# Attention of a two-layer hybrid encoder: lower probabilities on two 64-column halves of TensorE, scores without a rescale, late convolution taps added by DMA

## The chip, the core and the metric

The kernel runs on one core of a Trainium2 chip. TensorE (PE; PEld is its weight load), VectorE (DVE), ScalarE (ACT), GpSimd (POOL) and SyncE (SP, which issues DMAs) each run their own queue in order. The metric is the device time of one execution in microseconds. The median of three runs before is 2212.58 us (2212.55 to 2213.03).

## What is computed

Two layers, each with multi-head latent attention beside a convolution module, then a gated feed-forward part with a short convolution. 1024 tokens, width 1024, 8 heads, head sizes 64 (plain) + 32 (rotary) for queries and keys and 64 for values. What matters here:

```python
sc = einsum("bqhd,bkhd->bhqk", qn, k_nope) + einsum("bqhr,bkr->bhqk", qr, k_rope)
p = softmax(sc * scale)                 # scale = 1 / sqrt(96)
y_attn = einsum("bqhk,bkhd->bqhd", p, v)
u = a * sigmoid(gt)                     # the convolution module, beside attention
u = dwconv(u, w_dw_conv) + b            # 31 taps, per channel
u = silu(layernorm(u))
y = concat([y_attn, u]) @ w_o
```

## The kernel before

Channels lie on partitions, tokens along the free dimension. A float32 factor is held as two parts, an upper and a lower one, and a product of two factors is three matmuls (upper x upper, upper x lower, lower x upper). In attention the parts are float16.

A layer has three stages: the projection (`project`), attention (`attention`) with the output product behind it, and the feed-forward part. Each has its own PSUM pool; in attention there are two wide tiles of two banks for scores (`wide`) and four single banks (`bank`) for turned probabilities and for outputs.

**Scales.** In the projection, sums of squares of weights and gains give powers of two by which queries and keys are scaled before they become float16. `query_scale` and `key_scale` work each out from a column of `qk`, on DVE after a tiny matmul with ones; `head_squares` squares the query and key weights on ACT. `score_scale` makes the factor `self.sback` that brings a score back to its true size.

**Attention** is written as 64 units per layer, n = 8 * head + query tile of 128 tokens. Unit n issues, in this order:
- `values` (L1841): one of four chunks of 256 keys of a group of 512 queries. The stationary operand `v` is 128 columns wide: 64 columns of upper values and 64 of lower ones. The odd heads have them the other way round. So `v` times the upper probabilities gives upper x upper on one half of the output's partitions and lower x upper on the other. With the lower probabilities `pt[1]` it gives upper x lower and, unused by the three-matmul rule, lower x lower. Four matmuls of 512 columns (two blocks of 128 keys by two parts). After the fourth chunk both halves of the bank `o` are scaled and added into `yt` (L1847 on ACT, L1848 on DVE).
- `turn` (L1818): eight transposes of probabilities into PSUM tiles `t`; ACT writes the upper part (L1820), DVE the lower part (L1821).
- `scores` (L1777) for the tile two units ahead: six matmuls of 512 columns, then on DVE the negated row maximum `mx` (L1779), multiplied by `sback` (L1780).
- `expo` (L1788) for the tile one unit ahead: ACT takes the exponential with `mx` as its bias and `sback` as its scale, with the row sums beside it.
- `agenda[n]`: side work. Among it are row sums turned by a transpose of 8 columns (`sr`, L1859), weight casts for the output product, and the late taps.

**Taps.** Of the 31 taps of the four blocks of 128 convolution channels, some are done in the projection; 50 of the first layer and 49 of the second are left to attention (`late`). `LATE_KINDS` gives, by half of the list and in turns of five, how each is done (`tap_late`): "act": two halves on ACT (L2009), then a DMA that adds the result to `conv` (L2017); "pool": one product on POOL (L2012), then such a DMA; "both": a product and an addition on POOL (L2012, L2015), no DMA. The DMAs are issued by POOL. `LATE_COST` spreads the taps over the first 56 units; only the ACT halves are tied to a unit, POOL works through its queue as it can. An addition to one `conv` block waits for the one before it. `conv_total` (L2023, POOL) sums the blocks in units 57 to 59, `conv_split` (L2027, ACT and DVE) makes parts of the sum in unit 64, and `lnp` (L2039, PE) takes its mean behind attention.

Of the kernel before, what the change touches and what calls it, by code (L numbers as in the profile page):

```python
# [49 lines left out]
P_GQ = 8  # L50
# [31 lines left out]
MANUAL = [E.PE, E.DVE, E.Activation, E.Pool, E.SP]  # L82
LATE_KINDS = (("act", "both", "pool", "act", "pool"), ("pool", "both", "pool", "pool", "pool"))
LATE_COST = {"act": 1.1, "pool": 3.5, "both": 4.8}
# [54 lines left out]
class Encoder:  # L139
# [420 lines left out]
    def project(self, l, carry):  # L560
# [14 lines left out]
        def gain_squares():  # L575
            nc.vector.memset(col(6), 0.0)
            for i, at, n in ((0, P_GQ, 3), (4, P_GKV, 2)):
                nc.scalar.activation(out=self.blk(f"gsq{l}{i}")[:, 0:n], in_=par[:, at:at + n], func=AF.Square, accum_out=col(i))

        def head_squares(name):  # L580
            hi = w[name][0]
            i = {"u0": 1, "u1": 2, "u2": 3, "k": 5}[name]
            nc.scalar.activation(out=self.blk(f"hsq{l}{name}", F16, tuple(hi.shape)), in_=hi.bitcast(F32), func=AF.Square, accum_out=col(i))

        def totals(at, n, name):
            ps = self.bank(f"{name}{l}", (128, n))
            nc.tensor.matmul(ps, self.ones, col(at, n), start=True, stop=True)
            return ps

        def query_scale():  # L590
            sums = totals(0, 4, "qt")
            nc.vector.tensor_reduce(out=col(0), in_=sums[:, 1:4], op=ALU.add, axis=AX.X)
            nc.vector.tensor_tensor(out=col(0), in0=sums[:, 0:1], in1=col(0), op=ALU.mult)
            self.half_exponent(col(1), col(0))
            self.power(col(2), col(1), -1.0, 199.0)

        def score_scale():
            self.power(col(3), col(1), 1.0, 55.0)
            self.power(col(4), col(5), 1.0, 50.0)
            nc.vector.scalar_tensor_tensor(out=col(7), in0=col(3), scalar=SCALE, in1=col(4), op0=ALU.mult, op1=ALU.mult)  # L600
            self.sback = col(7)

        def key_scale():
            nc.vector.tensor_copy(out=col(4, 3), in_=totals(4, 3, "kt"))
            nc.vector.scalar_tensor_tensor(out=col(4), in0=col(4), scalar=float(KVL), in1=col(5), op0=ALU.mult, op1=ALU.mult)
            nc.vector.tensor_tensor(out=col(4), in0=col(4), in1=col(6), op=ALU.add)
            self.half_exponent(col(5), col(4))
            self.power(col(6), col(5), -1.0, 204.0)
            launch(key_rope_end())
# [93 lines left out]
        def queries_norm():  # L703
            r, d = self.blk(f"rq{l}"), rooted("qroot")
            st["rq"] = r
            query_scale()
# [156 lines left out]
        scales = {1: lambda: st.update(squares=self.weight_squares(l, w["v"])),  # L863
                  2: lambda: (st.update(scale=self.scales(l, st.pop("squares"))), score_scale())}
        for j in range(4):
# [9 lines left out]
        def supply(now, turn=TURN):  # L875
            while coming and coming[0][1] <= now + LEAD:
                name, at = coming.pop(0)
                turning.append((name, at, self.cast(l, name)))
            while turning and turning[0][1] <= now + turn:
                name, at, e = turning.pop(0)  # L880
                w[name] = self.complete(*e)
                if name in ("u0", "u1", "u2", "k"):
                    head_squares(name)
# [856 lines left out]
    def attention(self, l, u, conv, away, spill, kvs, loaded, ahead, wo, begun):  # L1740
# [28 lines left out]
        def scores(n):  # L1769
# [9 lines left out]
            nc.vector.tensor_reduce(out=mx, in_=ps, op=ALU.max, axis=AX.X, negate=True)  # L1779
            nc.vector.tensor_scalar(out=mx, in0=mx, scalar1=self.sback, scalar2=None, op0=ALU.mult)  # L1780
            st["s"][qt] = ps, mx

        def expo(n):
# [3 lines left out]
            p = self.tmp("b" if qt % 4 == 3 else "wr", f"p{l}_{h}_{qt}")  # L1787
            nc.scalar.activation(out=p, in_=ps, func=AF.Exp, bias=mx, scale=self.sback,  # L1788
                                 accum_out=st["sums"][:, qt:qt + 1])
# [36 lines left out]
        def values(group, c, n):  # L1826
# [11 lines left out]
            pt = st["pt"][gg][c // 2]  # L1838
            for s in range(2):
                for i in range(2):  # L1840
                    nc.tensor.matmul(po, v[2 * c + i][:, h // 2, e, :], pt[s][:, 2 * (c % 2) + i, :],  # L1841
                                     start=(c == 0 and i == 0 and s == 0), stop=(c == 3 and i == 1 and s == 1))
            if c < 3:
# [314 lines left out]
```

## Time and profile before

| | |
|---|---|
| profiled execution | 2213.27 us |
| its span | 2211.5 us |
| median of the runs | 2212.58 us |
| granted TensorE clock | 0.999 |
| projection of layer 0, until about | 198 us |
| attention of layer 0, steady part | 217.5 to 395.2 us |
| its end, until the first output products | 413.3 us |
| attention of layer 1 begins about | 1305 us |

In the page, a row of a group reads: line, engine, operation, output <- inputs by the program's names with buffer numbers left out, shapes, count, then busy time and mean duration of one, then idle time ahead and what ended it. A matmul's end is modelled, and it overlaps the next; what a matmul costs in a stream is the distance from start to start, and that is what the chain of waits shows. In a row of a time line, the first number is the start in microseconds from the start of the span, the second the length. The stage rows give busy time of PE, PEld, DVE, ACT and POOL, then the granted clock, the mean busy share of the 16 DMA engines and GB/s.

### The profile page before, as it was taken

How to read it: one execution, taken by the hardware profiler on the slowest of the kernel's cores; microseconds unless marked ns; L12 is line 12 of the kernel's file. 1: busy time of each engine (PE TensorE's matmuls, PEld its weight loads, DVE VectorE, ACT ScalarE, POOL GpSimd, SP SyncE). 2: the span in 40 equal slices, each digit the busy share in tenths (PEclk: the TensorE clock that was granted, in tenths of full speed). 3: DMA queues.
4: the chain of work that ended last, by engine and by line, in shares of the span. 5: the costliest groups of instructions: out<-in, count | busy, mean ns of one | idle time of the engine just before them, and what ended most of it. 6: DMA issues, size and time to landing. Idle time of an engine off the chain costs nothing.

```text
span 2211.5 us, 29902 instructions
## 1 busy us (share of the span) xinstructions
PE 2200.3 (99%) x10774; PEld 1320.3 (60%) x10774; DVE 1857.6 (84%) x2644; ACT 1487.9 (67%) x2223; POOL 593.5 (27%) x546
## 2 busy tenths in 40 slices
PE   9999999999999999999999999999999999999998
PEld 8887666784444444644488876667744444446445
DVE  6989999778988887787859789997788888878877
ACT  5455988745898886554623669887468987865544
POOL 1221799511111111000012227983111111110000
PEclk9999999999999999999999999999999999999999
DMA  6886878955588886554558958778646888856533
GB/s 192 164 178 176 161 159 160 289 142 120 126 249 258 221 258 160 191 167 154 166 137 166 194 148 174 157 178 241 167 103 146 257 238 238 239 141 220 183 117 120
DMA packets 163269, 400.96 MB, mean 181 GB/s; under 512 B 22144, under 2 KB 30192, under 8 KB 163120
## 3 DMA queue, kind: packets, MB, share of 16 engines
q0 software_dynamic: 67136, 154.28, 37.7%
q1 hardware_dynamic: 95696, 244.24, 32.3%
q8 instruction: 84, 1.38, 0.3%
q10 hardware_dynamic: 288, 0.53, 0.1%
q14 instruction: 65, 0.53, 0.1%
HBM read 270.75 MB, written 69.66 MB: 154 GB/s over the span
## 4 chain that ended last, share of the span: by engine, by line
PE 90%; DVE 6%; ACT 2%; issue 1%; DMA 1%; SPq 0%; DVEq 0%; ACTq 0%
PE p L1268 36%; PE pd L1513 16%; PE po L1002 7%; PE s L1777 7%; PE o L1841 5%; PE t L1818 5%; PE pa L239 2%; PE pg L239 2%; DVE conv L1995 2%; PE pg L557 2%; PE pq L239 1%; PE pkv L239 1%; PE pn L239 1%; PE pa L557 1%; PE pv L1753 1%
## 5 line engine op out<-in xcount | busy, mean ns | idle before, releaser
L1268 PE MATMUL p<-b,w 128*128 128x512 f16 x3696 | 804.0, 379 | 0.0
L1268 PEld LDWEIGHTS <-w 128*128 128x128 f16 x3696 | 361.5, 99 | 427.4 <-issue 1.1
L1513 PE MATMUL pd<-ab,wd 128*128 128x512 f16 (+2 forms) x1920 | 404.2, 373 | 0.0
L1159 POOL DMA_DIRECT2D wu<-in_w_up x176 | 152.9, 882 | 744.2 <-DVE w L1232 539.8
L1513 PEld LDWEIGHTS <-wd 128*128 128x128 f16 x1656 | 161.9, 98 | 179.3 <-issue 0.5
L1777 PE MATMUL s<-k,q 96*128 96x512 f16 x768 | 186.9, 379 | 0.0
L1232 DVE SCALAR_TENSOR_TENSOR w<-wu,wf,w 128x512 f16<-128x512 f32 (+1 forms) x216 | 177.3, 835 | 3.9 <-ACT w L1229 3.9
L1821 DVE SCALAR_TENSOR_TENSOR pt<-t,pt 128x512 f16<-128x512 f32 x256 | 163.4, 679 | 14.7 <-ACT pt L1820 11.5
L2012 POOL TENSOR_TENSOR late<-gate,par 128x1016 f32<-128x1016 f32 (+11 forms) x79 | 170.9, 2163 | 0.0
L1229 ACT ACTIVATE w<-wu,wf 128x512 f16<-128x512 f32 (+1 forms) x216 | 165.3, 784 | 0.0
L1820 ACT ACTIVATE pt<-t 128x512 f16<-128x512 f32 x256 | 139.4, 597 | 38.3 <-PE t L1818 36.7
L1788 ACT ACTIVATE p<-s,mx,qk 128x1024 f32<-128x1024 f32 x128 | 155.4, 1214 | 2.1 <-DVE mx L1780 1.1
L1779 DVE TENSOR_REDUCE mx<-s 128x1 f32<-128x1024 f32 x128 | 155.3, 1213 | 0.0
L1502 ACT ACTIVATE ab<-ac,ds 128x512 f16<-128x512 f32 x108 | 75.7, 718 | 108.2 <-DVE ac L1417 72.8
L1995 DVE SCALAR_TENSOR_TENSOR conv<-gate,par,conv 128x1009 f32<-128x1009 f32 (+14 forms) x110 | 139.9, 1275 | 3.3 <-ACT conv L657 0.6
L1818 PEld LDWEIGHTS t<-ident,p 128*128 128x128 f32 x1024 | 119.6, 141 | 28.5 <-ACT p L1788 2.1
L1818 PE MATMUL t<-ident,p 128*128 128x128 f32 x1024 | 134.4, 273 | 1.7 <-ACT p L1788 1.0
L1841 PE MATMUL o<-pt,v 128*128 128x512 f16 x512 | 131.3, 379 | 0.0
L1725 DVE SCALAR_TENSOR_TENSOR o<-zg,par,o 128x1023 f32<-128x1023 f32 x88 | 112.8, 1282 | 8.9 <-ACT o L1719 7.4
L1276 DVE SCALAR_TENSOR_TENSOR zg<-p,wf,zg 128x512 f32<-128x512 f32 x72 | 54.1, 751 | 72.2 <-PE p L1268 62.3
L1777 PEld LDWEIGHTS <-q 96*128 96x128 f16 x768 | 74.2, 97 | 64.6 <-issue 2.1
L1725 DVE SCALAR_TENSOR_TENSOR v<-zv,par,v 128x1023 f32<-128x1023 f32 x88 | 112.2, 1277 | 0.0
(2190 smaller groups left out, 3978.7 us busy)
## 6 DMA issues: line engine op xcount, KB each, us to landing
wu<-in_w_up SPq DMA_DIRECT2D x98, 512.0 KB
wu<-in_w_up POOLq DMA_DIRECT2D x176, 256.0 KB, 4.8
sd<-in_w_down SPq DMA_DIRECT2D x44, 512.0 KB
ws<-sd SPq DMA_DIRECT2D x44, 512.0 KB
act<-v SPq DMA_DIRECT2D x36, 512.0 KB
ac<-act SPq DMA_DIRECT2D x72, 256.0 KB
wo<-in_w_o POOLq DMA_DIRECT2D x64, 256.0 KB, 7.2
x_mix<-y SPq DMA_DIRECT2D x32, 256.0 KB
```

Source lines behind the costliest of these rows:

```text
L1229: nc.scalar.activation(out=t, in_=src, func=AF.Copy, scale=scale[f])
L1232: nc.vector.scalar_tensor_tensor(out=t, in0=src, scalar=scale[f], in1=hi, op0=ALU.mult, op1=ALU.subtract)
L1268: nc.tensor.matmul(ps, w[p][:, k * 128:(k + 1) * 128], b[:, q], start=(i in (1, 5, 2) and k == 0 and t == 0), stop=(k == 3 and t == 2), sk ...
L1513: nc.tensor.matmul(ps[t, m][:, cs], w[i, j][p][:, m * 128:(m + 1) * 128], b[:, q, cs], start=(i in (1, 5, 2) and j == 0 and s == 0), stop= ...
L1725: self.nc.vector.scalar_tensor_tensor(out=o[:, a:b], in0=z[:, at + a:at + b], scalar=self.par[l][:, tap:tap + 1], in1=o[:, a:b], op0=ALU.m ...
L1777: nc.tensor.matmul(ps[:, cs], q[0:96, i, qs], k[0:96, j, cs], start=(s == 0), stop=(s == 2))
L1788: nc.scalar.activation(out=p, in_=ps, func=AF.Exp, bias=mx, scale=self.sback, accum_out=st["sums"][:, qt:qt + 1])
L1818: nc.tensor.transpose(tp[:, i, qi * 128:(qi + 1) * 128], st["p"][2 * qp + qi][:, kt * 128:(kt + 1) * 128], self.ident)
L1821: nc.vector.scalar_tensor_tensor(out=lo, in0=tp, scalar=P_SCALE, in1=hi, op0=ALU.mult, op1=ALU.subtract)
L1841: nc.tensor.matmul(po, v[2 * c + i][:, h // 2, e, :], pt[s][:, 2 * (c % 2) + i, :], start=(c == 0 and i == 0 and s == 0), stop=(c == 3 and ...
L1995: self.nc.vector.scalar_tensor_tensor(out=y[:, lo:hi], in0=u[:, lo + s:hi + s], scalar=self.tap(l, j, t), in1=y[:, lo:hi], op0=ALU.mult, o ...
L2012: self.nc.gpsimd.tensor_tensor(out=p[:, lo:hi], in0=u[:, lo + s:hi + s], in1=self.tap(l, j, t).broadcast_to([128, hi - lo]), op=ALU.mult)
```

## The change

Three edits.

1. `values`: the two matmuls with the lower probabilities take only the 64 columns of upper values. The first block of 128 keys goes into partitions 0 to 63 of the bank, the second into 64 to 127. The lower x lower products are left out, and the upper x lower ones are spread over both halves, which are added at the end as before.
2. Queries are no longer scaled by a power of two of their own: `key_scale` also makes the factor `col(2)` for them, the keys' scale taken back and 1/sqrt(96) put in. The scores leave TensorE in their true size; `mx` is not multiplied, and the exponential has no scale. `query_scale`, `score_scale` and the squares of the three query weights go.
3. `LATE_KINDS`: in both halves of the list "both" becomes "pool"; in the second half the first of each five turns from "pool" to "act".

```diff
-LATE_KINDS = (("act", "both", "pool", "act", "pool"), ("pool", "both", "pool", "pool", "pool"))
+LATE_KINDS = (("act", "pool", "pool", "act", "pool"), ("act", "pool", "pool", "pool", "pool"))
...
-        def query_scale():
-            sums = totals(0, 4, "qt")
-            nc.vector.tensor_reduce(out=col(0), in_=sums[:, 1:4], op=ALU.add, axis=AX.X)
-            nc.vector.tensor_tensor(out=col(0), in0=sums[:, 0:1], in1=col(0), op=ALU.mult)
-            self.half_exponent(col(1), col(0))
-            self.power(col(2), col(1), -1.0, 199.0)
...
         def key_scale():
-            nc.vector.tensor_copy(out=col(4, 3), in_=totals(4, 3, "kt"))
+            sums = self.bank(f"kt{l}", (128, 3))
+            nc.tensor.matmul(sums, self.ones, col(4, 3), start=True, stop=True)
+            nc.vector.tensor_copy(out=col(4, 3), in_=sums)
...
-            self.power(col(6), col(5), -1.0, 204.0)
+            self.power(col(6), col(5), -1.0, 200.0)
+            self.power(col(2), col(5), 1.0, 54.0)
+            nc.vector.tensor_scalar(out=col(2), in0=col(2), scalar1=SCALE, scalar2=None, op0=ALU.mult)
...
             nc.vector.tensor_reduce(out=mx, in_=ps, op=ALU.max, axis=AX.X, negate=True)
-            nc.vector.tensor_scalar(out=mx, in0=mx, scalar1=self.sback, scalar2=None, op0=ALU.mult)
...
-            nc.scalar.activation(out=p, in_=ps, func=AF.Exp, bias=mx, scale=self.sback,
+            nc.scalar.activation(out=p, in_=ps, func=AF.Exp, bias=mx,
...
-            for s in range(2):
-                for i in range(2):
-                    nc.tensor.matmul(po, v[2 * c + i][:, h // 2, e, :], pt[s][:, 2 * (c % 2) + i, :],
-                                     start=(c == 0 and i == 0 and s == 0), stop=(c == 3 and i == 1 and s == 1))
+            for i in range(2):
+                nc.tensor.matmul(po, v[2 * c + i][:, h // 2, e, :], pt[0][:, 2 * (c % 2) + i, :],
+                                 start=(c == 0 and i == 0), stop=False, skip_group_check=True)
+            for i in range(2):
+                nc.tensor.matmul(po[i * 64:i * 64 + 64], v[2 * c + i][:, h // 2, e, main], pt[1][:, 2 * (c % 2) + i, :],
+                                 start=False, stop=(c == 3), skip_group_check=True)
```

On TensorE, one unit of values between scores and turns (first layer, head 0, second group; `pt_10` is a tile of lower probabilities; each matmul has a weight load ahead of it). Before:

```order
L1777 MATMUL s_1_1_1962<-k_1_1704,q_1_1703 128x512
L1841 LDWEIGHTS v_0_1608
L1841 MATMUL o_0_1_1976<-pt_00_1876,v_0_1608 128x512
...
L1841 MATMUL o_0_1_1976<-pt_10_1877,v_0_1608 128x512
...
L1818 MATMUL t_0_32_1981<-ident,p_0_6_1899 128x128 x2
L1818 MATMUL t_0_32_1981<-ident,p_0_7_1935 128x128 x2
```

And now:

```order
L1760 MATMUL s_1_1_1938<-k_1_1686,q_1_1685 128x512
L1822 LDWEIGHTS v_0_1593
L1822 MATMUL o_0_1_1949<-pt_00_1854,v_0_1593 128x512
...
L1825 MATMUL o_0_1_1949<-pt_10_1855,v_0_1593 64x512
...
L1800 MATMUL t_0_32_1954<-ident,p_0_6_1876 128x128 x2
L1800 MATMUL t_0_32_1954<-ident,p_0_7_1911 128x128 x2
```

The order and the number of matmuls stay (each `o` row stands twice, once per block of keys); those with `pt_10` write 64 partitions instead of 128.

On DVE, in the same stretch (`mx` the maximum, `pt_1x` the lower probabilities). Before:

```order
L1779 TENSOR_REDUCE mx_2_5_2412<-s_2_5_2405 128x1
L1780 TENSOR_SCALAR mx_2_5_2412<-mx_2_5_2412,qk_84 128x1
L1821 SCALAR_TENSOR_TENSOR pt_11_2326<-t_2_12_2429,pt_01_2325 128x2x256
L1821 SCALAR_TENSOR_TENSOR pt_11_2326<-t_2_13_2436,pt_01_2325 128x2x256
L1779 TENSOR_REDUCE mx_2_6_2450<-s_2_6_2443 128x1
L1780 TENSOR_SCALAR mx_2_6_2450<-mx_2_6_2450,qk_84 128x1
```

And now:

```order
L1803 SCALAR_TENSOR_TENSOR pt_11_2289<-t_2_13_2394,pt_01_2288 128x2x256
L1762 TENSOR_REDUCE mx_2_6_2408<-s_2_6_2401 128x1
L1845 RECIPROCAL rs_1_2419<-sr_1_2417 8x128
L1803 SCALAR_TENSOR_TENSOR pt_10_2433<-t_2_20_2427,pt_00_2432 128x2x256
L1803 SCALAR_TENSOR_TENSOR pt_10_2433<-t_2_21_2438,pt_00_2432 128x2x256
L1762 TENSOR_REDUCE mx_2_7_2452<-s_2_7_2445 128x1
```

The `TENSOR_SCALAR` behind each maximum is gone; nothing else moved.

On POOL, the first late taps of the first layer (`late_j_t` is tap t of block j, `conv_j` the sum). Before:

```order
L2012 TENSOR_TENSOR late_0_19_1758<-gate_0_416,par_63 128x1020
L2015 TENSOR_TENSOR conv_0_475<-conv_0_475,late_0_19_1758 128x1020
L2012 TENSOR_TENSOR late_1_19_1798<-gate_1_477,par_63 128x1020
L2017 DMA conv_1_539<-late_1_19_1798 128x1020
...
L2017 DMA conv_3_854<-late_3_17_1827 128x1022
L2012 TENSOR_TENSOR late_3_18_1903<-gate_3_786,par_63 128x1021
L2015 TENSOR_TENSOR conv_3_854<-conv_3_854,late_3_18_1903 128x1021
```

And now:

```order
L1996 TENSOR_TENSOR late_0_19_1739<-gate_0_414,par_63 128x1020
L2001 DMA conv_0_473<-late_0_19_1739 128x1020
L1996 TENSOR_TENSOR late_1_19_1742<-gate_1_475,par_63 128x1020
L2001 DMA conv_1_537<-late_1_19_1742 128x1020
...
L2001 DMA conv_3_852<-late_3_17_1806 128x1022
L1996 TENSOR_TENSOR late_3_18_1880<-gate_3_784,par_63 128x1021
L2001 DMA conv_3_852<-late_3_18_1880 128x1021
```

Each addition on POOL has become a DMA issue. Over both layers 79 such issues become 99, the 20 additions and 10 of the 79 products on POOL go, and the halves of taps on ACT go from 40 to 60.

More of the change, by code (lines that the diff above doesn't have):

```diff
@@ L576, in gain_squares @@
             nc.vector.memset(col(6), 0.0)
-            for i, at, n in ((0, P_GQ, 3), (4, P_GKV, 2)):
-                nc.scalar.activation(out=self.blk(f"gsq{l}{i}")[:, 0:n], in_=par[:, at:at + n], func=AF.Square, accum_out=col(i))
+            nc.scalar.activation(out=self.blk(f"gsq{l}")[:, 0:2], in_=par[:, P_GKV:P_GKV + 2], func=AF.Square, accum_out=col(4))
         def head_squares(name):
             hi = w[name][0]
[L582 to L588, printed above, removed]
-        def query_scale():
-            sums = totals(0, 4, "qt")
-            nc.vector.tensor_reduce(out=col(0), in_=sums[:, 1:4], op=ALU.add, axis=AX.X)
-            nc.vector.tensor_tensor(out=col(0), in0=sums[:, 0:1], in1=col(0), op=ALU.mult)
-            self.half_exponent(col(1), col(0))
-            self.power(col(2), col(1), -1.0, 199.0)
[L597 to L601, printed above, removed]
+            nc.scalar.activation(out=self.blk(f"hsq{l}{name}", F16, tuple(hi.shape)), in_=hi.bitcast(F32), func=AF.Square, accum_out=col(5))
         def key_scale():
-            nc.vector.tensor_copy(out=col(4, 3), in_=totals(4, 3, "kt"))
+            sums = self.bank(f"kt{l}", (128, 3))
+            nc.tensor.matmul(sums, self.ones, col(4, 3), start=True, stop=True)
+            nc.vector.tensor_copy(out=col(4, 3), in_=sums)
             nc.vector.scalar_tensor_tensor(out=col(4), in0=col(4), scalar=float(KVL), in1=col(5), op0=ALU.mult, op1=ALU.mult)
@@ L705, in queries_norm @@
             st["rq"] = r
-            query_scale()
             for s, p in zip(HALVES, self.spread(d, f"rq{l}", HALVES, self.bank)):
@@ L863, in project @@
         scales = {1: lambda: st.update(squares=self.weight_squares(l, w["v"])),
-                  2: lambda: (st.update(scale=self.scales(l, st.pop("squares"))), score_scale())}
+                  2: lambda: st.update(scale=self.scales(l, st.pop("squares")))}
         for j in range(4):
@@ L881, in supply @@
                 w[name] = self.complete(*e)
-                if name in ("u0", "u1", "u2", "k"):
+                if name == "k":
                     head_squares(name)
```

## The prediction

> **What bounds the kernel now.** I read the page's head and its chain first, then the chain of waits inside attention in order of time, then the busy time by stretch.
>
> ```profile
> span 2211.5 us, 29902 instructions
> PE 2200.3 (99%) x10774; PEld 1320.3 (60%) x10774; DVE 1857.6 (84%) x2644; ACT 1487.9 (67%) x2223; POOL 593.5 (27%) x546
> PE 90%; DVE 6%; ACT 2%; issue 1%; DMA 1%; SPq 0%; DVEq 0%; ACTq 0%
> ```
>
> TensorE is busy all the time and makes up 90% of the chain. So only work taken off TensorE can shorten this kernel, and only as long as nobody else falls behind. The change works on attention, so here is its chain in the first layer (start, length, engine and line):
>
> ```profile
> 217.68 0.88 PE t L1818 x6
> ...
> 301.58 1.30 PE s L1777 x6
> 302.87 0.87 PE o L1841 x4
> 303.74 0.87 PE t L1818 x8
> 304.61 1.30 PE s L1777 x6
> ...
> 395.24 0.91 PE t L1818 x8
> ```
>
> One unit of attention is scores (six matmuls, 1.30 us), values (four, 0.87) and turns (eight transposes, 0.87): 3.03 us, back to back, with no other engine in the chain. A streamed 512-column matmul thus costs 0.87/4 = 0.216 us. The busy time by stretch (PE, PEld, DVE, ACT, POOL, then clock, DMA share, GB/s; the last row is the values line alone, PE and PEld):
>
> ```profile
> 3.00:198.00 195.00, 194.44 (x878) 160.20 (x878) 167.61 (x211) 99.65 (x121) 39.71 (x48) 1.00 0.76 176
> 217.50:282.00 64.50, 64.33 (x378) 39.42 (x379) 60.15 (x93) 61.56 (x109) 50.91 (x35) 1.00 0.81 160
> 217.50:395.20 177.70, 177.53 (x1051) 109.45 (x1051) 167.49 (x256) 156.03 (x273) 154.31 (x103) 1.00 0.80 161
> 217.50:395.20 177.70, 59.92 (x232) 22.60 (x232) 1.00 0.80 161
> ```
>
> The steady stretch holds 232/4 = 58 units in 177.7 us, 3.06 each. The others are close behind: DVE 94%, ACT 95% up to 282, POOL 87%, DMA 0.80.
>
> **Values on two column halves.** The third and fourth product of a unit become two of 64 columns, one into partitions 0 to 63 of the bank, one into 64 to 127. If both stream together, four slots become three: 0.216 us a unit, 58 x 0.216 = 12.5 us a layer. No row of before shows two column tiles at once, so the saving lies between nothing and 0.216, and below nothing if switching between tile shapes costs. [...]
>
> ```profile
> 245.93 1.46 PE L1777 MATMUL s<-k,q 96*128 96x512 f16 x6
> 247.01 0.09 PEld L1859 LDWEIGHTS sr<-ident,sums 128*8 128x8 f32 x1
> 247.23 0.28 PE L1859 MATMUL sr<-ident,sums 128*8 128x128 f32 x1
> 247.23 0.64 PEld L1841 LDWEIGHTS <-v 128*128 128x128 f16 x4
> 247.34 1.02 PE L1841 MATMUL o<-pt,v 128*128 128x512 f16 x4
> ```
>
> Six scores from 245.93 at 0.216 end their streaming at 247.23, and the small tile starts right there; its weights were loaded at 247.01 under the last full matmul. The values start 0.11 later, what a transpose takes anyway (0.87/8). So neither switch costs anything that can be seen, and I put it at zero.
>
> [...]
>
> What is left is whether the second half's weights arrive in time. They are loaded as the first half's are; nothing of 64 columns is in the trace, so the load lies between these rows (mean ns behind the bar):
>
> ```profile
> L1859 PEld LDWEIGHTS sr<-ident,sums x14: 87/87/87, 247.0 to 1478.0; 128*8 128x8 f32 x14
> L1002 PEld LDWEIGHTS po<-us_0h,wo 128*128 128x128 f32 x64 | 12.0, 188 | 3.0 <-DVE wt L1180 0.7
> ```
>
> Between 87 ns for 8 columns and 188 for 128: by proportion 0.13 us. If both loads run under the second full product, the pair starts together. If the second load has to wait until the first half has started, the pair takes 0.216 + 0.13, and 0.086 us a unit is left. I take the first, as loads in the trace are always under the product ahead.
>
> [...]
>
> **Scores in true units.** The rescaling of the maximum goes. DVE, in a stretch where it does not wait:
>
> ```profile
> 305.30 1.29 DVE L1821 SCALAR_TENSOR_TENSOR pt<-t,pt 128x512 f16<-128x512 f32 x2
> 306.50 1.22 DVE L1779 TENSOR_REDUCE mx<-s 128x1 f32<-128x1024 f32 x1
> 307.75 0.21 DVE L1780 TENSOR_SCALAR mx<-mx,qk 128x1 f32<-128x1 f32 x1
> 307.88 1.28 DVE L1821 SCALAR_TENSOR_TENSOR pt<-t,pt 128x512 f16<-128x512 f32 x2
> ```
>
> From one pair to the next is 2.58 us, and every fourth unit has an eviction (`yt`) besides, 0.79 from its start to the next pair's, about 0.2 a unit: 2.78 before, against the new TensorE unit of 3.03 - 0.216 = 2.82. Without the rescaling the maximum and the pair take 1.20 each: 2.40 + 0.2 = 2.60. This edit saves nothing by itself, since TensorE covers it; it keeps DVE from being the next bound. In the projection, three squarings per layer on ACT, one tiny matmul and a chain of DVE scalars go. TensorE idles 0.56 us in that whole stage (first stretch above), so at most that: I take 0.1 a layer.
>
> **Late taps.** There are 50 a layer. Before: 10 on ACT, 30 on POOL, 10 on POOL with POOL's own addition; after: 15 and 35, all added by transfers. POOL and transfers, first layer:
>
> ```profile
> L2017 POOL DMA_DIRECT2D conv<-late x40: 847/888/1237, 215.8 to 380.2; - x40
> L2012 POOL TENSOR_TENSOR late<-gate,par x40: 1869/2188/2596, 216.4 to 377.7; 128x1014 f32<-128x1014 f32 x4, 128x1013 f32<-128x1013 f32 x4, 128x1012 f32<-128x1012 f32 x4, 128x1011 f32<-128x1011 f32 x4
> L2015 POOL TENSOR_TENSOR conv<-conv,late x10: 2326/2338/2362, 218.7 to 369.5; 128x1020 f32<-128x1020 f32 x1, 128x1021 f32<-128x1021 f32 x1, 128x1018 f32<-128x1018 f32 x1, 128x1017 f32<-128x1017 f32 x1
> q0 software_dynamic: 5529, 19.98, 65.6%
> q1 hardware_dynamic: 1936, 5.53, 13.5%
> ```
>
> POOL loses 10 x 2.34 + 5 x 2.19 and gains 10 x 0.89: 25 us less of 154. The queue rows are of 217.5 to 380. In these 162.5 us q0 is nearly the additions alone: 0.656 x 162.5 = 107 us of all 16 engines, 107/39 = 2.73 each. Fifty need 137, and q1 another 22: 159 us. With units of 2.82 to 2.86 the 55 units until the late taps are due end some 11 us earlier, near 369, 153 us after the first issue. So the transfers come out 6 us too long, and their end moves into the next stage.
>
> ACT gains five taps of two halves in the second half of attention, where it has room. In the first half it keeps its ten:
>
> ```profile
> 230.16 0.69 ACT L1847 ACTIVATE yt<-o,sc 64x512 f32<-64x512 f32 x1
> 230.87 1.09 ACT L1820 ACTIVATE pt<-t 128x512 f16<-128x512 f32 x2
> 233.18 0.71 ACT L2009 ACTIVATE late<-gate,par 128x512 f32<-128x512 f32 x1
> 233.79 1.07 ACT L1820 ACTIVATE pt<-t 128x512 f16<-128x512 f32 x2
> 236.58 0.60 ACT L1820 ACTIVATE pt<-t 128x512 f16<-128x512 f32 x1
> ```
>
> A unit with a half tap takes 236.58 - 233.79 = 2.79, of which the tap is 0.61; `yt` adds some 0.8 every fourth unit, 0.2 on the mean. Twenty halves over 25 units: 2.18 + 0.2 + 0.49 = 2.87, 0.05 over TensorE's 2.82. There ACT becomes the bound: 25 x 0.05 = 1.2 us a layer. Afterwards ten halves over 30 units: 2.58, free.
>
> At the end of attention the order is: last late tap, casts of the output weights, their completion, the first output products:
>
> ```profile
> 380.16 0.89 POOL L2017 DMA_DIRECT2D conv<-late  x1 [0.30 <-POOL late L2012]
> 380.74 1.97 POOL L964 DMA_DIRECT2D wo<-in_w_o  x3
> 389.70 0.90 POOL L203 DMA_DIRECT2D wo<-in_w_o  x1 [1.18 <-ACT wo L202]
> 400.24 0.47 PE L1002 MATMUL po_e<-ys_1h,wo 128*128 128x512 f32 x1
> ```
>
> The products come 10.5 us after the completion is issued; I allow about half of that as slack, so of the transfers' 6 us some 2 reach TensorE; all 6 and none are the ends.
>
> **The sum**, for a layer: -12.5 (values), -0.4 (the blocks of eight values at the end, which mostly wait for others), -0.1 (projection), +1.2 (ACT), +2.3 (transfers) = -9.5. Twice: -19. The profiled execution took 2213.3 us, its span 2211.5; that makes 2194, and the median of the runs, 2212.6, is only 0.7 lower. At the ends of the known costs: -13 x 2 gives 2187, -5.8 x 2 gives 2202.
>
> **Rivals.**
> - The second half's load is not hidden: 0.086 us x 58 x 2 = -10, no ACT term, little from transfers: 2204. For it: 64-column loads are in no row. Against: loads are hidden everywhere else.
> - Transfers set the length: they ran from 217 to 380.7 before, 163.5 us, and need 159: -4.5 a layer and -0.4, 2203. For it: 0.80 now and 25% more additions. Against: the additions may end late without anyone waiting.
> - The halves stream one after the other: four slots as before, 2213 less at most 1; the change then does not do what it says. Nothing in the trace speaks for or against.
> - Slower: each switch of tile shape drains TensorE. A matmul is 1.46 - 5 x 0.216 = 0.38 us long and streams for 0.216, so a drain is 0.16; two per unit cost 0.33 and save 0.216: +0.11 x 116 units = +13, 2226. It decides from 0.108 us a switch on. Against it stands the row-sum transpose, whose switches are free. [...]
>
> **How the numbers follow.** Forecast 0.58, unhidden load 0.12, transfers 0.10, no overlap 0.08, drain 0.10, something else 0.02. The first three are 0.80 and span 2185 to 2208, the range, with a few us for the sizes. A measurement here tells about 0.2%, 4.4 us, from no change: faster 0.80, same 0.09, slower 0.11.
>
> **What will show it.** Values at 0.65 us a unit in the chain and units near 2.85 show the overlap; 0.87 none; 0.78 a late load; over 1.0 a drain. The two half products of a unit should start within 0.02 us. ACT ahead of `t` in the chain before about 290 shows its term; additions landing after 376 and a wait of POOL or TensorE for them show the transfers. The forecast is wrong above all if the halves don't overlap.

## The result and the profile after

The changed kernel takes **2214.58 us** (2214.25 to 2215.0, 12 runs); beside it the kernel before took 2212.8 (2212.5 to 2213.64, 12 runs). The ratio is 1.0008, 95% interval 1.0 to 1.0015: no change that this measurement can tell from none. 2194 was forecast, faster, with a range of 2185 to 2208; the time lies outside it. The profiled execution has a span of 2213.0 us against 2211.5.

The head of the page and the shares of the chain:

```profile
span 2213.0 us, 29901 instructions
...
PE 97%; DVE 1%; ACT 1%; issue 0%; DVEq 0%; ACTq 0%
```

TensorE was 90% of the chain and is now 97% (experiment 8 below, without the halves and the taps, has 97% too). The chain leads less through the other engines, and yet nothing was gained. The chain of waits inside attention, in order of time (start, length, engine, line):

```profile
302.19 0.43 PE o L1822 x2
302.63 0.34 PE o L1825 x2
302.96 1.02 PE t L1800 x8
303.99 1.30 PE s L1760 x6
```

Values take 0.77 instead of 0.87, less than the four slots of before and more than three. But the turns behind them, the same eight transposes as before, take 1.02 instead of 0.87. The unit is 3.09 where it was 3.03. By the prediction's own signs 0.78 in the values' row meant a late load and over 1.0 a drain; as half of the price stands in the turns' row, that row alone would have misled. The time line of that unit, with the weight loads (bracket: how long the engine was idle before, and what ended it):

```profile
302.03 0.60 PE L1822 MATMUL o<-pt,v 128*128 128x512 f16 x2
...
302.56 0.11 PEld L1825 LDWEIGHTS <-v 128*64 128x64 f16 x2 [0.42 <-issue]
302.56 0.41 PE L1825 MATMUL o<-pt,v 128*64 128x512 f16 x2
302.89 0.86 PEld L1800 LDWEIGHTS t<-ident,p 128*128 128x128 f32 x8 [0.23 <-issue]
302.89 1.09 PE L1800 MATMUL t<-ident,p 128*128 128x128 f32 x8
```

The same place in the kernel before:

```profile
302.50 0.75 PEld L1841 LDWEIGHTS <-v 128*128 128x128 f16 x4
302.71 1.03 PE L1841 MATMUL o<-pt,v 128*128 128x512 f16 x4
...
303.36 1.01 PEld L1818 LDWEIGHTS t<-ident,p 128*128 128x128 f32 x8
303.58 1.04 PE L1818 MATMUL t<-ident,p 128*128 128x128 f32 x8
```

Two things are to be seen. The two half products stand in one row of 0.41 us, the length of a single one (403 ns): they start 3 ns apart and stream together. And the weight loads stop being early: PEld idles 0.42 us ahead of the 64-column loads and 0.23 ahead of the next full ones, with nothing named that released it. Before, the loads ran some 0.2 us ahead of their products, under the product ahead. Call it a visit when TensorE goes to the 64-column shape and comes back. At all 128 visits, going and coming back, the first load of the new shape starts within 5 ns of its own product; ahead of the half products PEld is idle for 54.3 us in all:

```profile
L1825 PEld LDWEIGHTS <-v x256: 106/106/106, 218.8 to 1508.8; 128*64 128x64 f16 x128
L1825 PE MATMUL o<-pt,v x256: 403/403/403, 218.8 to 1508.8; 128*64 128x512 f16 x128
...
  issue: 54.3, 128
```

From start to start, in the nanoseconds of the trace, a unit now reads: second full product to first half 307 (a slot is 215 to 216, so 92 too many), half to half 3, second half to the first transpose 334 (118 too many), first to second transpose 165 (109 in a stream, so 56 too many). I read two kinds of loss in these numbers. On each way some 92 ns pass in which TensorE starts nothing, as if it had to empty. And the first product of the new shape carries its own weight load, since that starts only with it: the halves last 403 ns instead of 378, and the first transpose 328 instead of 273. The ends of matmuls are modelled, so this split is a reading; the distances from start to start are not. They add up to 92 + 3 on the way in and 93 + 25 and 56 on the way back: 0.27 us, where the slot saved is worth 0.216. The difference, 0.05, is what the unit is longer by (3089 ns against 3036 by the median).

### The profile page after: what moved, and what is told of

It is laid out like the page before. It is cut to its first block, busy times and chain, and to the rows that moved or that the text cites. A ratio compares the mean times of both kernels' runs of the same rounds, so it can differ in the third digit from the quotient of the medians.

```text
span 2213.0 us, 29901 instructions
## 1 busy us (share of the span) xinstructions
PE 2203.6 (100%) x10770; PEld 1299.8 (59%) x10770; DVE 1832.7 (83%) x2506; ACT 1481.1 (67%) x2227; POOL 545.6 (25%) x536
## 4 chain that ended last, share of the span: by engine, by line
PE 97%; DVE 1%; ACT 1%; issue 0%; DVEq 0%; ACTq 0%
PE p L1251 36%; PE pd L1496 17%; PE po L985 7%; PE s L1760 7%; PE t L1800 6%; PE pq L239 3%; PE pa L239 3%; PE o L1822 3%; PE pkv L239 2%; PE pg L239 2%; PE o L1825 2%; PE pg L557 2%; PE pn L239 1%; PE pk L239 1%; PE pa L557 1%; PE pv L1736 1%
## 5 line engine op out<-in xcount | busy, mean ns | idle before, releaser
L1996 POOL TENSOR_TENSOR late<-gate,par 128x1019 f32<-128x1019 f32 (+12 forms) x69 | 154.7, 2242 | 0.0
L1770 ACT ACTIVATE p<-s,mx 128x1024 f32<-128x1024 f32 x128 | 143.4, 1121 | 1.2 <-DVE mx L1762 0.8
L1800 PE MATMUL t<-ident,p 128*128 128x128 f32 x1024 | 139.7, 279 | 0.6 <-ACT p L1770 0.6
L1800 PEld LDWEIGHTS t<-ident,p 128*128 128x128 f32 x1024 | 110.5, 140 | 29.5 <-issue 26.4
L2001 POOL DMA_DIRECT2D conv<-late x99 | 87.3, 909 | 158.8 <-ACT late L1993 75.6
```

Source lines behind the costliest of these rows:

```text
L1800: nc.tensor.transpose(tp[:, i, qi * 128:(qi + 1) * 128], st["p"][2 * qp + qi][:, kt * 128:(kt + 1) * 128], self.ident)
L1996: self.nc.gpsimd.tensor_tensor(out=p[:, lo:hi], in0=u[:, lo + s:hi + s], in1=self.tap(l, j, t).broadcast_to([128, hi - lo]), op=ALU.mult)
```

## The experiments

All beside runs of the kernel before on the same chip, 2213.0 to 2213.4 us by the median in each set.

**1. The change without the halves.**

```diff
-            for i in range(2):
-                nc.tensor.matmul(po, v[2 * c + i][:, h // 2, e, :], pt[0][:, 2 * (c % 2) + i, :], ...)
-            for i in range(2):
-                nc.tensor.matmul(po[i * 64:i * 64 + 64], v[2 * c + i][:, h // 2, e, main], pt[1][:, 2 * (c % 2) + i, :], ...)
+            for s in range(2):
+                for i in range(2):
+                    nc.tensor.matmul(po, v[2 * c + i][:, h // 2, e, :], pt[s][:, 2 * (c % 2) + i, :], ...)
```

> The changed kernel with the values as before (four full-width products a unit); the scores in true units and the late taps by transfers stay. Theory (the two edits beside the halves are covered by TensorE; the switch of tile shape ate the gain): a unit of attention is back at 3.03 to 3.06 us, the projection keeps its 1.4 us, the transfers' larger share (about 0.95) makes nobody wait: 2210 to 2212.5. Rival (the transfers or the late taps on ScalarE hold attention, and the halves did gain): units longer than 3.06 and 2216 or more.

Measured: 2208.94 us, ratio 0.9981 (0.9972 to 0.9989). That is less than was expected. The two other edits gain 4.4 us, and the halves lose 5.6 on top of them (6.2 if each kernel is set against the runs of before beside it).

**2. The halves alone.** The kernel before with the new `values` and nothing else.

```diff
-            for s in range(2):
-                for i in range(2):
-                    nc.tensor.matmul(po, v[2 * c + i][:, h // 2, e, :], pt[s][:, 2 * (c % 2) + i, :], ...)
+            for i in range(2):
+                nc.tensor.matmul(po, v[2 * c + i][:, h // 2, e, :], pt[0][:, 2 * (c % 2) + i, :], ...)
+            for i in range(2):
+                nc.tensor.matmul(po[i * 64:i * 64 + 64], v[2 * c + i][:, h // 2, e, main], pt[1][:, 2 * (c % 2) + i, :], ...)
```

> The kernel before with the halves alone. Theory (each switch between full-width and 64-column products empties TensorE): full product to first half 0.31 us, last half to the next turn 0.33 us as in the changed kernel, a unit 3.09 us against 3.05, so 2.5 us a layer more: 2216 to 2219, later than the changed kernel because the projection's 1.4 us are not saved. Rival (the halves gain and the other edits lose it): 2195 to 2205.

Measured: 2218.86 us, ratio 1.0025 (1.0015 to 1.0034), 5.5 us more than before. The halves cost the same with and without the other edits, and the distances in the trace are within 1 ns those of the changed kernel (308, 3, 334, 165 ns). It is a price on TensorE itself, not one of engines that fall behind.

**3. Both half products on the same column half.** Both write partitions 0 to 63.

```diff
-                nc.tensor.matmul(po[i * 64:i * 64 + 64], v[2 * c + i][:, h // 2, e, main], pt[1]...
+                nc.tensor.matmul(po[0:64], v[2 * c + i][:, h // 2, e, main], pt[1]...
```

> The changed kernel with both half products of a unit on the same 64 columns, partitions 0 to 63, so that they cannot stream together; the sum of both halves of the bank is the same. Theory (cost per switch of shape, wherever the 64 columns lie): the two intervals at the switches stay at 0.31 and 0.33 us, the second half follows the first after 0.22 us with its load hidden, a unit 3.31 us, 2239 to 2243. Rival (the cost comes from loading the second column position or from loads of 64 columns as such): the intervals at the switches fall to 0.22 (only the second position cost), or each half product takes 0.31 (loads of 64 columns cannot be hidden), a unit 3.40 us and 2250.

Measured: 2242.49 us, ratio 1.0132 (1.0117 to 1.0148). Against the changed kernel that is 27.9 us in 128 visits, 0.22 each: one slot. The overlap in the changed kernel is therefore real and worth a whole slot. The time line of TensorE:

```profile
304.86 0.60 PE L1822 MATMUL o<-pt,v 128*128 128x512 f16 x2
305.39 0.62 PE L1825 MATMUL o<-pt,v 128*64 128x512 f16 x2
305.94 1.10 PE L1800 MATMUL t<-ident,p 128*128 128x128 f32 x8
306.87 0.81 PE L1760 MATMUL s<-k,q 96*128 96x512 f16 x3
```

The way in (0.53 from the first full product, 0.43 + 0.10) and the long turns (0.93) stay although only one column position is used. The price hangs on the width of the tile, not on two positions at once. The second half follows the first after 240 ns, 24 over a slot, and the first transpose follows it after 310, 94 over a slot. That bears out the split above by starts alone: some 25 for the load that the first half carries, some 92 for the way back.

**4. Three full-width products in a unit.** What the halves would give if the switch were free. It leaves out the lower probabilities of every second block of 128 keys.

```diff
+            for s, i in ((0, 0), (0, 1), (1, 0)):
+                nc.tensor.matmul(po, v[2 * c + i][:, h // 2, e, :], pt[s][:, 2 * (c % 2) + i, :], ...)
```

> The changed kernel with three full-width products a unit and no halves; it leaves out the lower probabilities of every second block of 128 keys. This is TensorE's time as I had forecast it for the halves, without a switch. If the other terms of the forecast hold (ScalarE 2.87 us a unit in the first 25 units, transfers 2 us a layer): units of 2.82 to 2.87 us, 2191 to 2195. If the transfers set the length of attention: 2203. If another engine cannot follow at all: 2208 or more.

Measured: 2187.91 us, ratio 0.9885 (0.9871 to 0.9898). Busy time by stretch (PE, PEld, DVE, ACT, POOL, then clock, DMA share, GB/s):

```profile
217.50:282.00 64.50, 64.16 (x381) 39.57 (x380) 59.08 (x77) 62.63 (x114) 44.28 (x35) 1.00 0.96 191
217.50:380.00 162.50, 162.01 (x967) 100.79 (x966) 150.71 (x193) 151.02 (x272) 126.47 (x95) 1.00 1.00 202
```

TensorE stays full while ACT runs at 97% of the first stretch and the transfers at 1.00. The 25 units from 219.9 us take 2.90 each and the next 29 take 2.86, against 2.82 without any wait; the last late addition is issued at 367.5, 20.5 us before the first output product (20.1 before the change). So the other engines and the transfers could follow, with a loss of a few us. With a free switch the gain would have been there, and larger than forecast; the 4.4 us of experiment 1 are part of it.

**5 and 6. One visit to the 64-column shape for two units, and for four.** The full-width products of upper probabilities stay where they are; the half products wait for the second, or the fourth, chunk of a block.

```diff
-            for i in range(2):
-                nc.tensor.matmul(po[i * 64:i * 64 + 64], v[2 * c + i][:, h // 2, e, main], pt[1][:, 2 * (c % 2) + i, :], ...)
+            for k in ((c - 1, c) if c % 2 else ()):        # 5;   6: (range(4) if c == 3 else ())
+                for i in range(2):
+                    nc.tensor.matmul(po[i * 64:i * 64 + 64], v[2 * k + i][:, h // 2, e, main],
+                                     st["pt"][gg][k // 2][1][:, 2 * (k % 2) + i, :], ...)
```

> The changed kernel, but the half products of two units of values are issued together with the second of them (four upper products full width in two units as now, then four half products in a row). Theory: the price belongs to the switch of tile shape, entry and return together 0.275 us, and is paid once per visit, however long the visit is. Two units then save 0.432 and pay 0.275: -0.157 x 29 visits x 2 layers = -9 from the 2209 of the version without halves, 2200; if each load between the half products shows 0.03 to 0.06 us, 2203 to 2204. In the trace 308 ns from the last full product to the first half, 3 ns between the halves of a pair, and 0.33 us to the next transposes, once in two units. Rival: the price belongs to each half product (0.14 us each, from loads of 64 columns that aren't hidden); then two units pay as much as now and the time is that of the changed kernel, 2214.6.

> As the last, but all eight half products of a block of values are issued together with its fourth unit. Theory (price per visit): four units save 0.864 and pay 0.275, less 0 to 0.18 for loads between the pairs: -0.59 to -0.41 x 29 = -17 to -12 from 2209, so 2192 to 2197. Rival (price per half product): 2214.6 again. A second rival: the uneven units (three of 2.6 us, one of 3.7) make DVE, at 2.6 us a unit, the bound of the short ones; then the gain is smaller than with pairs by two, 2200 to 2205.

Measured: 2198.53 us by two, ratio 0.9932 (0.9918 to 0.9945); **2195.91 us** by four, ratio 0.992 (0.9907 to 0.9934). Both beat the kernel before and the changed one. By two, on TensorE:

```profile
301.79 0.60 PE L1822 MATMUL o<-pt,v 128*128 128x512 f16 x2
302.22 1.03 PE L1800 MATMUL t<-ident,p 128*128 128x128 f32 x8
303.09 1.46 PE L1760 MATMUL s<-k,q 96*128 96x512 f16 x6
304.39 0.60 PE L1822 MATMUL o<-pt,v 128*128 128x512 f16 x2
304.92 0.62 PE L1826 MATMUL o<-pt,v 128*64 128x512 f16 x4
305.47 1.09 PE L1800 MATMUL t<-ident,p 128*128 128x128 f32 x8
306.40 1.46 PE L1760 MATMUL s<-k,q 96*128 96x512 f16 x6
```

The unit without half products takes 2.60 and its turns 0.87; the other takes 3.31, and only there stand the long way in (0.53) and the long turns (0.93). Four half products take 0.55 to the next transpose: two slots of 0.216, one load of some 0.02 and one way out; the second pair starts 240 ns after the first. Against experiment 1 the 64 visits gain 10.4 us, 0.163 each, where 0.157 was expected from 2 x 0.216 - 0.275. A price per half product would have given 2214.6. The price belongs to the visit.

By four, 32 visits gain 13.0 us, 0.41 each, at the lower end of what was expected. On TensorE, with one weight load:

```profile
304.63 1.34 PE L1800 MATMUL t<-ident,p 128*128 128x128 f32 x8
...
305.10 0.64 PEld L1800 LDWEIGHTS t<-ident,p 128*128 128x128 f32 x6 [0.32 <-ACT p L1770]
...
305.81 1.46 PE L1760 MATMUL s<-k,q 96*128 96x512 f16 x6
...
310.53 1.05 PE L1826 MATMUL o<-pt,v 128*64 128x512 f16 x8
311.51 0.65 PE L1800 MATMUL t<-ident,p 128*128 128x128 f32 x4
```

Eight half products take 0.98 to the next transpose; their pairs start 240, 216 and 216 ns apart, so only the first pair carries its load. But of three short units in a row some now have turns that wait: 1.18 us from 304.63 to 305.81 instead of 0.87. The second rival of that expectation had DVE as the bound of such units. The trace has ACT: here, and at the six other turns of the first layer that are late by over 0.12 us, a transpose starts 0.14 us behind the end of an exponential (L1770).

**7 and 10. What counts as a switch.** Both are experiment 1 with twelve small extra products that nobody reads, each between full-width scores and full-width values, where the row-sum transpose `sr` stands too. They have 8, 32, 64 or 128 columns.

```diff
+        def extra(h, w):                       # w = 8, 32, 64, 128, 64, 32 by head
+            x = self.bank(f"x{l}_{h}", (w, 128))
+            if l == 0:                         # 7: f32 transpose;   10: plain f32 product
+                nc.tensor.transpose(x, self.ident[:, 0:w], self.ident)
+            else:                              # 7: f16 product;     10: transpose of 16-bit data
+                nc.tensor.matmul(x, v[0][:, 0, 0, 0:w], v[0][:, 0, 0, :], start=True, stop=True)
```

> The version without halves (2209) with twelve small extra products whose result nobody reads, each between full-width scores and full-width values as the row-sum transpose is: in the first layer f32 transposes of the identity with 8, 32, 64, 128, 64 and 32 columns, in the second layer f16 products with as many columns. Time 2209 to 2213. It asks why the row-sum transpose showed no drain. Theory: every change of tile shape drains the array, and the row-sum transpose only seemed free: then scores to the extra product is 0.30 us at 8, 32 and 64 columns and 0.22 at 128, and from it to the values 0.20 or more against 0.11, in both layers. Rival A: f32 transposes are exempt: no gap in the first layer, gaps in the second. Rival B: narrow tiles of 8 and 32 columns are exempt, only 64 columns show gaps. Rival C: no gap anywhere; then the drain comes with the second column position or with the accumulation into one bank, not with the shape.

> The version without halves (2209) with twelve small extra products whose result nobody reads, between full-width scores and full-width values; this time f32 products that are not transposes in the first layer, and transposes of 16-bit data in the second, each with 8, 32, 64, 128, 64 and 32 columns. Time 2209 to 2213. The first probe had f32 transposes (no gap at any width: 216 ns from the scores to the extra product, 113 on to the values) and f16 products (309 and 152 to 176 at 8 to 64 columns, 216 and 60 at 128), so kind and type went together. Theory: the type decides: f32 products show 216 and about 113 at every width, 16-bit transposes 309 and 150 to 176 below 128 columns. Rival: transposing decides: f32 products show gaps below 128 columns, 16-bit transposes none.

Measured, in one run each: 2211.17 and 2213.56 us, and from start to start in ns (a full slot ahead is 216; for 128 columns there is no change of shape):

| extra product | scores to it, 8 to 64 columns | at 128 | from it to the values, 8 / 32 / 64 columns | at 128 |
|---|---|---|---|---|
| f32 transpose | 215 to 216 | 216 | 114 / 113 / 114 | 113 |
| f16 product | 309 | 216 | 152 / 163 / 176 | 60 |
| f32 product (two passes) | 309 | 216 | 205 / 205 / 205 after the second pass | 109 |
| transpose of 16-bit data | 309 to 310 | 215 | 153 / 163 / 178 | 63 |

So rival A of the first expectation holds: f32 transposes are exempt, f16 products are not. The rows of the first probe on TensorE, 64 columns as an f32 transpose, then as an f16 product. In each the scores end 0.216 after the start of their last one:

```profile
296.65 1.24 PE L1760 MATMUL s<-k,q 96*128 96x512 f16 x5
297.72 0.28 PE L1843 MATMUL x<-ident 128*64 128x128 f32 x1
297.84 1.03 PE L1823 MATMUL o<-pt,v 128*128 128x512 f16 x4
...
1392.77 1.03 PE L1760 MATMUL s<-k,q 96*128 96x512 f16 x4
1393.73 0.24 PE L1845 MATMUL x<-v 128*64 128x128 f16 x1
1393.90 1.04 PE L1823 MATMUL o<-pt,v 128*128 128x512 f16 x4
```

Five scores from 296.65 end at 297.73, and the f32 transpose starts at 297.72: free. Four from 1392.77 end at 1393.63, and the f16 product starts at 1393.73: 0.1 too late, and the values 0.17 behind it instead of 0.06 at 128 columns. Of the second probe, a plain f32 product of 64 columns, which runs as two passes:

```profile
297.19 1.24 PE L1760 MATMUL s<-k,q 96*128 96x512 f16 x5
298.36 0.43 PE L1843 MATMUL x<-ident 128*64 128x128 f32 x2
298.72 1.04 PE L1823 MATMUL o<-pt,v 128*128 128x512 f16 x4
```

The f32 product pays too: 1.17 from the first of five scores instead of 1.08, and 0.36 to the values, where the two passes of 128 columns take 0.22 (114 + 109 ns). So both ideas of that expectation fall: it is neither the type alone nor the transposing alone. Of the four kinds tried only the f32 transpose is exempt, at every width. That is the kind of `sr`, whose 14 starts in the kernel before read the same: 215 to 216 ns from the last scores to it, 113 to 114 from it to the values. Why this kind is exempt, no run shows.

**8 and 9. The two other edits, each alone.** The kernel before with the scores in true units, and the kernel before with the late taps all added by transfers.

```diff
-LATE_KINDS = (("act", "pool", "pool", "act", "pool"), ("act", "pool", "pool", "pool", "pool"))
+LATE_KINDS = (("act", "both", "pool", "act", "pool"), ("pool", "both", "pool", "pool", "pool"))
```

is experiment 8, on top of experiment 1, and the same two lines the other way round are experiment 9, on the kernel before.

> The kernel before with the scores in true units and nothing else of the change. It splits the 4.4 us that the two other edits gained without the halves (2208.9 against 2213.3). Theory: DVE, 0.2 us a unit lighter, no longer comes late for the turned banks, which before let TensorE wait here and there by 0.1 to 0.2 us: 2209 to 2210. Rival: the gain comes from the late taps, POOL's lighter load and its transfers: 2213 here.

> The kernel before with all late taps added by transfers and nothing else of the change. With and without this edit the version in true units took the same time (2208.94 both), so the theory is that it does nothing to the time: 2213.4, within 1 us. Rival A, the step of the prediction that charged 2.3 us a layer to the transfers: with units of 3.05 the transfers have 163 us and need 159, so here too some of it should show, 2215 to 2218. Rival B: POOL, 25 us lighter, was a hidden brake: 2209 to 2211.

Measured: 2208.94 us for the true units, ratio 0.998 (0.9971 to 0.9989), and 2212.89 for the late taps, ratio 1.0 (0.9991 to 1.0009). The whole 4.4 us comes from the true units. By stage starts the first layer gains 1.2 us up to the first values, 0.7 in attention and 0.6 between the first output product and `lnp`; the second layer repeats it with 0.6, 0.6 and 0.6. The kernel before, in the projection, in attention and at the output product, and the mean of its exponentials:

```profile
174.96 0.28 PE L587 MATMUL qt<-qk,ones_r 128*128 128x4 f32 x2
175.10 1.30 PE L316 MATMUL rq0s<-ident,rq0y 128*128 128x128 f32 x8
176.16 0.71 PE L239 MATMUL pu<-cqs_0h,wu20h 128*128 128x512 f32 x2
...
233.98 0.21 DVE L1780 TENSOR_SCALAR mx<-mx,qk 128x1 f32<-128x1 f32 x1
...
234.75 1.21 ACT L1788 ACTIVATE p<-s,mx,qk 128x1024 f32<-128x1024 f32 x1
...
236.10 0.64 PEld L1818 LDWEIGHTS t<-ident,p 128*128 128x128 f32 x6 [0.22 <-ACT p L1788]
...
402.81 1.38 PE L1818 MATMUL t<-ident,p 128*128 128x128 f32 x8 [0.24 <-DVE yt L1848]
404.31 0.62 PE L316 MATMUL rc_1s<-ident,rc 128*128 128x128 f32 x4
...
L1788 ACT ACTIVATE p<-s,mx,qk 128x1024 f32<-128x1024 f32 x128 | 155.4, 1214 | 2.1 <-DVE mx L1780 1.1
```

And the version in true units:

```profile
174.97 1.03 PE L316 MATMUL rq0s<-ident,rq0y 128*128 128x128 f32 x8
175.76 0.70 PE L239 MATMUL pu<-cqs_0h,wu20h 128*128 128x512 f32 x2
...
400.57 1.16 PE L1800 MATMUL t<-ident,p 128*128 128x128 f32 x8
401.85 0.62 PE L316 MATMUL rc_1s<-ident,rc 128*128 128x128 f32 x4
...
L1770 ACT ACTIVATE p<-s,mx 128x1024 f32<-128x1024 f32 x128 | 143.6, 1122 | 1.2 <-DVE mx L1762 0.8
```

In the projection the tiny product `qt` is gone and `pu` starts 0.4 us sooner; another tiny product, `sc0p`, starts at 192.19 instead of 192.96, which is 0.36 more.

In attention of the first layer eight starts of TensorE were late before by over 15 ns, 0.75 us in all, and two are late now, 0.12. At 236.10 a turn waits for an exponential. That one began at 234.75, when ACT was through with its own evictions (233.79 + 1.07, a row of the prediction); the rescaled maximum had been ready since 234.19. So at this place the rescale on DVE was not what TensorE waited for. But the edit also takes the scale out of the exponential, and with it the mean falls from 1214 to 1122 ns (experiment 9, which keeps the scale, has 1214). Two products of values that were 0.15 us late before, at 257.03 and 269.32, are 0.06 late now: 0.09 less, as much as an exponential is shorter.

In the output stage the rescale may count. The exponential at 399.96 started 0.09 behind the rescaled maximum, and the maximum alone was ready 0.33 before it; now it starts 0.03 behind the maximum. The profile, though, names a product of values as what ended ACT's idle time there. The turn that waited 0.24 for DVE no longer waits, and its eight transposes take 1.28 to the next product instead of 1.50. The shorter exponential and the missing rescale come with one edit, and no run has one without the other; how the 4.4 us divides between them stays open.

## Why the prediction was wrong

**What bounds the kernel** was right in the main: TensorE, back to back, and taking a slot out of each unit shortens the kernel (experiment 4). That only work taken off TensorE can shorten it was too strong, as the true units show below.

**That the halves stream together** was right: 3 ns apart, and 27.9 us are lost when they don't (experiment 3).

**That the switch of tile shape is free** is the step that failed, and with it the sign of the largest term. It was put at zero on one row, the transpose of the row sums, read as a small tile between full ones. Experiments 7 and 10 show that the row was no instance of the thing at all: f32 transposes do not pay at any width, and every other kind does. The price is some 92 ns on each way, and 81 (25 + 56) for the two loads that nothing hides: 0.27 us, once for a whole visit (experiments 5 and 6), against 0.216 saved in a visit of one pair. Instead of -12.5 us a layer, the halves gave +3.1 from the first values product to the first output product (183.0 against 179.9 in experiment 1).

The rival that had this mechanism, each switch draining TensorE, gave 0.16 for a switch. That was the author's estimate, the modelled length of a matmul less its slot (0.38 less 0.216), and no run shows it; measured are 0.27 for both ways where it had 0.33, and of these only 0.185 can be draining, if the split above is right; the rest are loads. Its time, 2226, was too long by that difference and by the gain of the true units; its chance, 0.10, was too small because of the one row.

**That the 64-column load is hidden** was wrong as well. Its length was about right, 0.106 for the 0.13 estimated, but by luck: the two rows that it was put between are f32 loads, and `v` is f16, whose 128-column loads take 0.098, less than the 64-column ones. No load, of either shape, was pulled under a product of the other shape: at all 128 visits it starts with its own product. The second half's load, which had a rival of its own, hid beside the first half's; what shows is 25 ns for the pair, and 56 for the full-width load on the way back.

**That true units save nothing by themselves** was wrong by 4.4 us. The reasoning looked at DVE alone, 2.78 a unit beside TensorE's 3.03, and DVE does have room. It left out that the exponential loses its scale too and is 0.09 us shorter on ACT, the engine that the turn at 236.10 waited for; and it took a mean load for proof that nobody waits. For the projection it allowed 0.1 a layer, and at most the 0.56 for which TensorE was idle there; 0.4 at `qt` and 0.36 at `sc0p` are more than that, since the tiny product itself went with the waits.

**Late taps.** The transfers' +2.3 us a layer did not come: the edit alone changes nothing (experiment 9), and even at a share of 1.00 the last addition was issued as long before the output products as before the change (experiment 4). The amount was sized well: between 217.5 and 380 us the queue of these additions went from 65.6% to

```profile
q0 software_dynamic: 6958, 25.13, 82.8%
```

28 us more for ten additions, 2.8 each where 2.73 was used. What failed is the step from transfers that end later to a TensorE that waits. ACT's +1.2 us a layer could not show at units of 3.09. Its sum also has the exponential at its old length: with 0.09 less, the 2.87 a unit is 2.78, under TensorE's 2.82. In experiment 4 the first 25 units are 0.04 longer than the next 29, 1.0 us, of the size that was charged; what of it is ACT's was not separated.

**The blocks of eight** gain 0.6 us a layer, but the same with the true units alone; the halves give nothing there (11.72 us from the first output product to `lnp`, 11.70 in experiment 1).

**The sum, as measured:** 2213.3 - 4.4 (true units, experiment 8) + 0 (late taps, experiment 9) + 5.5 (halves, experiment 2) = 2214.4, where the whole change took 2214.6.

## What to carry to other kernels

Count the visits to another tile shape, not the products in it. Here each pair of half products saved a slot of 0.216 us, and going there and back cost some 0.27 in a visit of one pair as of two (0.432 - 0.163): against experiment 1 one pair to a visit lost 5.6 us, two gained 10.4, and four, with some turns waiting for ACT, 13.0. So gather narrow products until a visit saves several slots. Before a row is used as evidence that something is free, make sure that it is an instance of the thing: same kind of instruction, same type, same shape. And when an edit removes an operand or a step, compare the mean length of every group that it touches, on all engines: here the exponential became 0.09 us shorter on an engine that TensorE waited for, and the prediction had looked at another.

## What was not expected of the hardware

- Going from 128 columns to fewer took TensorE 92 to 94 ns on the way in, whatever the width (8, 32 or 64 columns), for an f16 product, an f32 product and a transpose of 16-bit data (309 to 310 from start to start where 215 to 216 is a slot, experiments 7 and 10; 307 in the changed kernel). On the way back it was 92 ns at 8 columns and 116 at 64 for the f16 product (152 and 176 against 60, experiment 7). I read the 24 between them as the load that the narrow product carries: the half products, which carry one, last 403 ns instead of 378.
- f32 transposes of 8, 32 and 64 columns cost nothing of this: 215 to 216 ns ahead, 113 to 114 behind, where 128 columns have 216 and 113 (experiment 7).
- A 64-column load of `v` in f16 took 106 ns, a 128-column one 95 to 101 (changed kernel).
- Two products of 64 columns and 512 streamed ones, on the two column positions, start 3 ns apart and take the time of one (0.41 us for the pair, 403 ns for one, changed kernel); a second pair on the same two positions starts 240 ns after the first, 24 over a slot, and a third and fourth 216 after the one ahead (experiment 6).
- An exponential of 128x1024 f32 took 1214 ns on ACT with its scale from a column (before, and experiment 9), and 1122 without a scale (experiment 8).
